# Two-layer hybrid block on one core: the next norm two tiles behind the update, other weight places and product order in the last groups, and norms in place

## The chip, the cores and the metric

One NeuronCore of one Trainium2 chip runs the whole program. The metric is the device time of one execution in microseconds (us). A core has five engines with queues of their own: PE (TensorE, matrix products), DVE (VectorE), ACT (ScalarE), POOL (GpSimd) and SP (SyncE, which here issues every DMA). [...] PE's clock stands at one of two levels, which the profile shows as a granted clock of 1.0 or 0.5.

## The reference

The input is 1024 tokens of width 1024, everything in float32. Each of two layers computes a mixer and an MLP, both with adaptive norms:

```
mod = cond @ w_ada[l] + b_ada[l]; sh_m, sc_m, g_m, sh_f, sc_f, g_f = split(mod, 6)
h = rmsnorm(x, norm_g[l, 0]) * (1 + sc_m) + sh_m
y = hybrid_mixer(h, ...)            # three attention-like branches, joined, @ w_out
x = x + g_m * rmsnorm(y, norm_g[l, 1])
h = rmsnorm(x, norm_g[l, 2]) * (1 + sc_f) + sh_f
y = square(relu(h @ w_up[l])) @ w_down[l]        # 1024 -> 4096 -> 1024
x = x + g_f * rmsnorm(y, norm_g[l, 3])
```

A norm of a token needs the sum of squares over its 1024 columns, so it is a reduction, a reciprocal root and a product.

## The kernel before

**Arithmetic.** A float32 product is made of three PE matmuls (`mm3`, lines 191 to 193): each operand is cut into a high part (a cast, mostly on ACT) and a low part (what is left, a subtraction, mostly on DVE), and high·high, high·low and low·high are added up in PSUM. `split` (lines 234 and 235) makes the two parts of a weight or an activation.

**Order of the work.** The kernel is written as Python generators that are woven together (`weave`), and a scheduler at build time then sets each engine's instruction order from the data dependences, the order written and its own timeline. On the chip each engine takes its queue strictly in order. SP issues the DMAs in order too; a DMA whose target is not yet free holds up all behind it.

**Memory.** Three kinds of space matter. The arena F (`Arena`, about 17 slabs of 128x1024 words) holds loads and intermediate tiles; a slab can be filled again when its last reader is done. The tile R is cut into slots ("places") of 2x1024 columns for split operands: in the down projection `load` takes places from the list `free`, in other stages R holds the normed and transposed input `hT` (slots 8 to 15). PSUM is used as named banks: `bank_s` with two buffers in the down projection, `bank_t` for transposes there, `bank_b` in the projections.

**Stages of a layer.** Eight token tiles of 128 tokens, t = 0 to 7. The mixer ends with `out_proj` per tile (load of x, line 1296; sum of squares; product; line 1302 stores x) and `renorm` per tile: load x (line 1317) into one slab, square it into a second slab u (line 613), the norm product into u (line 614), then transposes on PE and splits into `hT` (lines 620, 621, or 210 to 235 in `transp_late` for tiles 4 to 7, which also forms the sums that the up projection uses). Tiles 6 and 7 keep their x on the chip (`kept`). The up projection `mlp_up` works on weight columns in 16 blocks: six "lead" loads of 128 columns (`plain`) run while tiles 4 to 7 are still being normed; then come loads of 256 columns (line 269), whose sums POOL forms (lines 277 to 283) and `split` cuts, five products each (`sums`).

**The down projection** (`mlp_down`) goes through the 32 slices of 128 rows in groups, `GROUPS = [2] + [4] * 6 + [2, 4]`. For each slice of a group it loads and splits a piece of the activations and a piece of the weights (two places), then for each tile multiplies all slices of the group into one PSUM tile of two halves and adds that to y[t] (line 386; in the last group the last tile in halves, line 381). Group 7 has two slices (four places) and group 8, the last, four slices (eight places). Before either of them the list `free` is sorted.

**The end of a layer** is in `finish` of `run` (line 1498) and `finish` of the class: for each tile of the last group a square on ACT (line 666), the reciprocal root (lines 182 to 186), a product on DVE (line 667), the residual addition on POOL (line 668) and the store. Tile 7 goes in halves, with the addition on DVE (lines 656 to 664). In layer 0 the norm for layer 1 follows the addition: square (line 613 again), root, product (line 614), then the transposes (lines 641 and 630). `load_w` (lines 693 and 694) splits the first weights of layer 1 for the queries and keys; their projection is the first `bank_b` product of the layer. The names `fss` and `nss` in the rows are the sums of squares of the finish and of the norm.

## Time and profile before

| what | us |
|---|---|
| median of three runs (lowest, highest) | 2834.05 (2823.96, 2837.48) |
| the profiled execution | 2822.46 |
| its span in the trace | 2820.4 |
| PE busy in it | 2621.0 |
| DVE busy in it | 1747.9 |
| ACT busy in it | 1134.2 |
| POOL busy in it | 576.7 |

The rows of the trace give a start and a duration in us from the span's start. A number in square brackets at a row's end is the idle time of that engine just before, with the engine and line that ended it. Matmuls overlap: one of 512 columns is shown with 0.39 us, but the next one starts 0.23 later at full clock. Where a row says x8, eight instructions are merged, and its duration runs from the first start to the last end. In the profiled execution layer 0's down projection ends near 1459, layer 1's mixer near 2090, and its down projection near 2812.

### The profile page before, as it was taken

To read this page: it belongs to the slowest core of one execution; us is meant where nothing else is said; L and a number is where in the kernel's file an instruction comes from. 1 tells how busy PE (TensorE), PEld (TensorE's weight loads), DVE (VectorE), ACT (ScalarE), POOL (GpSimd) and SP (SyncE) were. 2 spreads that over 40 slices of the span, in tenths; PEclk is the share of its full clock that TensorE was granted. 3 is DMA by queue.
4 is the path that set the end of the run, shared out by engine and by line. 5 is a ranking of instruction groups with operands and counts; after the bars stand their busy time and mean duration, and the time that the engine had idled before them with its cause. 6 is when DMAs were issued, how large, how long until landed. Compare 5 with 4: busy or idle time off the path is not lost. (4 is left out here: it accounts for less than half of the span.)

```text
span 2820.4 us, 34988 instructions
## 1 busy us (share of the span) xinstructions
PE 2621.0 (93%) x12530; PEld 2048.1 (73%) x12530; DVE 1747.9 (62%) x3351; ACT 1134.2 (40%) x2265; POOL 576.7 (20%) x509
## 2 busy tenths in 40 slices
PE   5799998898799999999979999979987999999998
PEld 4677776675677777777768777657765888888886
DVE  7767676643887777576574667754458555543435
ACT  5243443544544445121153434444446455621112
POOL 1441243210143320000021113341002433000002
PEclk9899999998999999999989999879998999999999
DMA  6441312313255547353240222231132433531303
GB/s 226 116 137 49 96 60 77 98 62 104 79 185 172 160 158 236 129 166 116 78 148 22 64 84 66 61 119 60 59 120 83 146 116 112 194 134 60 120 30 120
DMA packets 268529, 311.55 MB, mean 110 GB/s; under 512 B 28674, under 2 KB 212164, under 8 KB 268356
## 3 DMA queue, kind: packets, MB, share of 16 engines
q1 hardware_dynamic: 268356, 309.32, 34.0%
q8 instruction: 99, 1.62, 0.2%
q14 instruction: 74, 0.61, 0.1%
HBM read 242.85 MB, written 66.43 MB: 110 GB/s over the span
## 5 line engine op out<-in xcount | busy, mean ns | idle before, releaser
L191 PE MATMUL bank_b<-split 128*128 128x512 f32 (+2 forms) x1824 | 722.9, 397 | 47.1 <-ACT split L234 28.1
L192 PE MATMUL bank_b<-split 128*128 128x512 f32 (+2 forms) x1824 | 707.5, 388 | 0.2 <-DVE split L694 0.2
L193 PE MATMUL bank_b<-split 128*128 128x512 f32 (+2 forms) x1824 | 704.8, 388 | 1.2 <-DVE split L636 1.2
L234 ACT CAST split<-arena_f 128x512 fp32r<-128x512 f32 (+1 forms) x384 | 281.8, 761 | 630.9 <-PE bank_s L192 385.9
L191 PE MATMUL bank_s<-split 128*128 128x512 f32 (+2 forms) x1152 | 454.1, 397 | 17.9 <-ACT split L1061 4.7
L192 PE MATMUL bank_s<-split 128*128 128x512 f32 (+2 forms) x1152 | 450.8, 391 | 9.6 <-DVE split L235 6.7
L193 PE MATMUL bank_s<-split 128*128 128x512 f32 (+2 forms) x1152 | 448.2, 389 | 0.0
L191 PEld LDWEIGHTS bank_b<-split 128*128 128x128 f32 x1824 | 352.5, 193 | 126.9 <-ACT split L234 32.2
L235 DVE TENSOR_TENSOR split<-arena_f,split 128x512 fp32r<-128x512 f32 (+1 forms) x384 | 355.2, 941 | 89.7 <-ACT split L234 88.2
L193 PEld LDWEIGHTS bank_b<-split 128*128 128x128 f32 x1824 | 350.7, 192 | 68.4 <-issue 3.1
L192 PEld LDWEIGHTS bank_b<-split 128*128 128x128 f32 x1824 | 352.4, 193 | 63.8 <-issue 3.9
L386 DVE TENSOR_TENSOR arena_f<-arena_f,bank_s 128x1024 f32<-128x1024 f32 x126 | 153.5, 1219 | 248.4 <-PE bank_s L193 248.2
L191 PEld LDWEIGHTS bank_s<-split 128*128 128x128 f32 (+1 forms) x1152 | 218.1, 190 | 73.5 <-issue 5.8
L192 PEld LDWEIGHTS bank_s<-split 128*128 128x128 f32 (+1 forms) x1152 | 218.9, 190 | 56.8 <-DVE split L235 9.0
L193 PEld LDWEIGHTS bank_s<-split 128*128 128x128 f32 (+1 forms) x1152 | 218.9, 190 | 44.3 <-issue 0.8
L869 ACT ACTIVATE arena_f<-bank_s,nm 128x128 f32<-128x128 f32 (+3 forms) x192 | 141.9, 741 | 188.6 <-DVE nm L868 155.2
L868 DVE TENSOR_REDUCE nm<-bank_s 128x1 f32<-128x128 f32 (+3 forms) x192 | 141.5, 751 | 106.2 <-PE bank_s L1083 62.1
L548 DVE SCALAR_TENSOR_TENSOR arena_f<-arena_f,cond 128x128 f32<-128x128 f32 x448 | 155.9, 376 | 50.5 <-DMA arena_f<-in_w_ada 20.7
L897 ACT COPY arena_f<-bank_t 128x512 f32<-128x512 f32 (+1 forms) x160 | 86.7, 542 | 108.9 <-PE bank_t L894 97.9
L668 POOL TENSOR_TENSOR arena_f<-arena_f 128x1024 f32<-128x1024 f32 x14 | 34.5, 2461 | 460.9 <-DVE arena_f L667 453.9
L250 ACT ACTIVATE arena_f<-arena_f 128x512 f32<-128x512 f32 x128 | 80.8, 632 | 113.7 <-DVE arena_f L324 52.5
L881 PE MATMUL bank_a<-arena_f 128*64 128x256 f32 (+1 forms) x640 | 108.3, 399 | 19.2 <-ACT arena_f L897 15.0
(280 smaller groups left out, 3260.1 us busy)
## 6 DMA issues: line engine op xcount, KB each, us to landing
arena_f<-in_w_ada SPq DMA_DIRECT2D x80, 512.0 KB
d_r<-arena_f SPq DMA_DIRECT2D x128, 256.0 KB
arena_f<-in_w_up SPq DMA_DIRECT2D x32, 1024.0 KB
arena_f<-in_w_down SPq DMA_DIRECT2D x64, 512.0 KB
arena_f<-d_r SPq DMA_DIRECT2D x64, 512.0 KB
arena_f<-d_x SPq DMA_DIRECT2D x36, 512.0 KB
d_x<-arena_f SPq DMA_DIRECT2D x23, 512.0 KB
arena_f<-in_w_in SPq DMA_DIRECT2D x20, 512.0 KB
```

Of the source, the lines that this page charges most:

```text
L191: mm(out, wh, xh, start=start, stop=False)
L192: mm(out, wh, xl, start=False, stop=False)
L193: mm(out, wl, xh, start=False, stop=stop)
L234: self.nc.scalar.copy(hi, src)
L235: (eng or self.nc.vector).tensor_sub(lo, src, f32(hi))
L250: nc.scalar.activation(t, t, AF.Relu)
L386: nc.vector.tensor_add(y[t], y[t], ps)
L548: nc.vector.scalar_tensor_tensor(acc, in0=w[:, k], scalar=self.cond[:, k:k + 1], in1=acc, op0=ALU.mult, op1=ALU.add)
L868: nc.vector.tensor_reduce(nm, S[:, 0:n], axis=AX.X, op=ALU.max, negate=True)
L869: nc.scalar.activation(p[:, 0:n], S[:, 0:n], AF.Exp, bias=nm, accum_out=ls)
L881: nc.tensor.matmul(bk[jj * 64:jj * 64 + 64, 128 * half:256], v[:, 2 * c + jj], e[:, 256:384] if half else e[:, jj * 256:jj * 256 + 256], s ...
L897: nc.scalar.copy(held, ps[:, 0:w])
```

## The change

Three parts. In `mlp_down` the two sorts of `free` give other places to the last two groups: group 7 now takes 0, 1, 6, 7, and group 8 takes 2, 3, 4, 5 first and then 0, 1, 6, 7; and in the last group the products of tiles 6 and 7 run as first slices of 6, first slices of 7, last slices of 6, last slices of 7. In `run` the finish of tile t is written ahead of the norm, and the norm is that of tile t-2 instead of t-1. In `renorm` x is loaded into u itself and normed there, and the squares, which nobody reads, go to a free part of R; tiles 6 and 7 hand over their two slabs.

```
@@ -365,20 +365,35 @@
             last = f0 == FF // P
             if f0 + GROUPS[-1] >= FF // P:
 
-                free.sort()
+                free.sort(key=lambda i: (i > 7, i in (0, 1, 6, 7)) if last else (i > 7, 1 < i < 6))
             rw = []
             for f in fs:
                 rw.append((load(self.d_r[l][f]), load(w_dn[f * P:(f + 1) * P, :])))
-            for t in range(NT):
+            banks = {}
+
+            def products(t, ns, tip=False):
                 tok = slice(t * P, t * P + P)
-                ps = self.bank2()
-                tip = last and t == NT - 1
+                ps = banks[t] = banks.get(t) or self.bank2()
                 for dh in range(2):
                     dd = slice(dh * 512, dh * 512 + 512)
-                    for n, ((_, r), (_, wd)) in enumerate(rw):
+                    for n in ns:
+                        r, wd = rw[n][0][1], rw[n][1][1]
                         self.mm3(ps[:, dd], r[:, 0, tok], r[:, 1, tok], wd[:, 0, dd], wd[:, 1, dd], n == 0, n == size - 1)
                     if tip:
                         nc.vector.tensor_add(y[t][:, dd], y[t][:, dd], ps[:, dd])
+
+            for t in range(NT):
+                tip = last and t == NT - 1
+                if not last or t < NT - 2:
+                    products(t, range(size))
+                elif not tip:
+
+                    for tt in (t, t + 1):
+                        products(tt, range(size // 2))
+                    products(t, range(size // 2, size))
+                else:
+                    products(t, range(size // 2, size), True)
+                ps = banks[t]
                 if g == 0:
                     y.append(F.get(D, top=True))
                     nc.scalar.copy(y[t], ps)
@@ -606,11 +621,14 @@
         return t
 
 
-    def norm(self, x, a, xn):
+    def norm(self, x, a, xn, junk=None):
 
         nc = self.nc
         ss = self.sm(1, "nss")
-        nc.scalar.activation(xn, x, AF.Square, accum_out=ss)
+        if junk is None:
+            nc.scalar.activation(xn, x, AF.Square, accum_out=ss)
+        else:
+            nc.scalar.activation(junk, x.rearrange("p (a k q) -> p a k q", a=2, q=P), AF.Square, accum_out=ss)
         nc.vector.scalar_tensor_tensor(xn, in0=x, scalar=self.rstd(ss), in1=a, op0=ALU.mult, op1=ALU.mult)
 
     def cut_cols(self, ps, b, hi, lo):
@@ -1300,23 +1318,24 @@
         nc.vector.scalar_tensor_tensor(u, in0=u, scalar=rs, in1=g, op0=ALU.mult, op1=ALU.mult)
         nc.vector.tensor_add(x, x, u)
         nc.sync.dma_start(dst[t * P:t * P + P], x)
-        F.put(u)
         if keep is None:
+            F.put(x, u)
+        else:
+            keep[t] = x, u
+
+    def renorm(self, t, src, nxt, hT):
+
+        F = self.F
+        if type(src) is dict:
+            x, u = src[t]
+            self.norm(x, nxt[0], u)
             F.put(x)
         else:
-            keep[t] = x
-
-    def renorm(self, t, src, nxt, hT):
-
-        F = self.F
-        u = F.get(D)
-        if type(src) is dict:
-            x = src[t]
-        else:
-            x = F.get(D)
-            self.nc.sync.dma_start(x, src[t * P:t * P + P])
-        self.norm(x, nxt[0], u)
-        F.put(x)
+
+            u = F.get(D)
+            self.nc.sync.dma_start(u, src[t * P:t * P + P])
+            h = self.R[:, 8 * SLOT:16 * SLOT].rearrange("p (a k t) -> p a k t", a=2, k=KD)
+            self.norm(u, nxt[0], u, h[:, :, 4:8, t * P:t * P + P])
         yield 1.0
         if t < 4:
             self.transp8(u, hT[0], hT[1], t, True, nxt[1])
@@ -1504,14 +1523,14 @@
                         tail["w"] = list(self.stage_w(I["w_in"][l + 1], self.qk_cols(0), 2))
                 if more and t == NT - 1:
                     tail["w0"] = self.load_w(tail["w"], 2)
+                if t < NT:
+                    self.finish(y[t], self.d_x[2 * l], tail["g"], o, t, tail["x"][t % 3], y[t],
+                                hT[0][:, :, t * P:t * P + P])
+                if more and t > 1:
+                    self.norm(tail["x"][(t - 2) % 3], tail["nxt"][0], y[t - 2])
                 if more and 2 < t < 7:
                     self.transp8(y[t - 3], hT[0], hT[1], t - 3, False, tail["nxt"][1])
                     F.put(y[t - 3])
-                if more and 0 < t <= NT:
-                    self.norm(tail["x"][(t - 1) % 3], tail["nxt"][0], y[t - 1])
-                if t < NT:
-                    self.finish(y[t], self.d_x[2 * l], tail["g"], o, t, tail["x"][t % 3], y[t],
-                                hT[0][:, :, t * P:t * P + P])
 
             bg = iter(())
             if more:
@@ -1525,6 +1544,7 @@
                 F.put(tail["g"])
                 if more:
                     finish(NT)
+                    finish(NT + 1)
                     for t in range(4, NT):
                         self.transp8(y[t], hT[0], hT[1], t, True, tail["nxt"][1])
                         F.put(y[t])

```

Line numbers move: in the rows of the changed kernel 401 and 383 are what 386 and 381 were, 685 is 667, 632 is 614, 639 is 621, 712 is 694, 680 and 681 are 662 and 663, 1336 is 1317, 1314 and 1320 are 1296 and 1302.

On DVE, at the end of layer 0, where tiles 2 and 3 are added. L386 (401) adds the products to y, L667 (685) is the product of the finish, L614 (632) that of the norm; the `rstd` names tell which root a product uses. Before:

```order
L186 TENSOR_SCALAR rstd_y_10688<-rstd_t_10690,rstd_y_10688 128x1
L386 TENSOR_TENSOR arena_f<-arena_f,bank_s 128x1024
L186 TENSOR_SCALAR rstd_y_10700<-rstd_t_10702,rstd_y_10700 128x1
L614 SCALAR_TENSOR_TENSOR arena_f<-arena_f,rstd_y_10688 128x1024
L667 SCALAR_TENSOR_TENSOR arena_f<-arena_f,rstd_y_10700 128x1024
L386 TENSOR_TENSOR arena_f<-arena_f,bank_s 128x1024
```

The norm product of tile 0 stands ahead of the finish product of tile 1, behind the add of tile 2. The same place with the change:

```order
L186 TENSOR_SCALAR rstd_y_10729<-rstd_t_10731,rstd_y_10729 128x1
L186 TENSOR_SCALAR rstd_y_10742<-rstd_t_10744,rstd_y_10742 128x1
L685 SCALAR_TENSOR_TENSOR arena_f<-arena_f,rstd_y_10729 128x1024
L632 SCALAR_TENSOR_TENSOR arena_f<-arena_f,rstd_y_10742 128x1024
L401 TENSOR_TENSOR arena_f<-arena_f,bank_s 128x1024
```

The finish product is now that of tile 2, one tile further on, and the norm product of tile 0 follows right behind it, ahead of the add of tile 3.

On SP, at the seam from the mixer to the up projection of layer 1. `d_x` is x in memory, `in_w_up` the weights: 128x8x128 a lead load, 128x8x256 a load for the sums; `d_r` takes the up projection's results. Before:

```order
L1317 DMA arena_f<-d_x_106 128x1024 x3
L1296 DMA arena_f<-d_x_105 128x1024 x2
L1317 DMA arena_f<-d_x_106 128x1024
L269 DMA arena_f<-in_w_up 128x8x128 x3
L1317 DMA arena_f<-d_x_106 128x1024
L1302 DMA d_x_106<-arena_f 128x1024
L269 DMA arena_f<-in_w_up 128x8x128
L1302 DMA d_x_106<-arena_f 128x1024
L252 DMA d_r_110<-arena_f 128x512 x2
L269 DMA arena_f<-in_w_up 128x8x128 x2
L252 DMA d_r_110<-arena_f 128x512 x3
L269 DMA arena_f<-in_w_up 128x8x256
```

The last two lead loads stand behind two stores of results, and the first load for the sums behind three more. With the change:

```order
L269 DMA arena_f<-in_w_up 128x8x128
L1314 DMA arena_f<-d_x_105 128x1024
L1336 DMA arena_f<-d_x_106 128x1024 x2
L1314 DMA arena_f<-d_x_105 128x1024
L1336 DMA arena_f<-d_x_106 128x1024 x2
L269 DMA arena_f<-in_w_up 128x8x128 x2
L1320 DMA d_x_106<-arena_f 128x1024
L269 DMA arena_f<-in_w_up 128x8x128
L1320 DMA d_x_106<-arena_f 128x1024
L269 DMA arena_f<-in_w_up 128x8x128
L252 DMA d_r_110<-arena_f 128x512 x2
L269 DMA arena_f<-in_w_up 128x8x128
```

Five of the six lead loads now stand ahead of the first store of results, and directly behind the sixth follow two loads for the sums.

On DVE, at the end of the kernel, where tile 6 is finished and tile 7 is added in halves (L381, with the change L383). Before:

```order
L386 TENSOR_TENSOR arena_f<-arena_f,bank_s 128x1024
L183 TENSOR_SCALAR rstd_m_20456<-fss_20453 128x1
L381 TENSOR_TENSOR arena_f<-arena_f,bank_s 128x512
L184 RECIPROCAL rstd_y_20455<-rstd_y_20455 128x1
L185 TENSOR_SCALAR rstd_t_20457<-rstd_y_20455,rstd_m_20456 128x1
L186 TENSOR_SCALAR rstd_y_20455<-rstd_t_20457,rstd_y_20455 128x1
L667 SCALAR_TENSOR_TENSOR arena_f<-arena_f,rstd_y_20455 128x1024
L381 TENSOR_TENSOR arena_f<-arena_f,bank_s 128x512
```

The first half of tile 7 is added in the middle of tile 6's finish. With the change:

```order
L401 TENSOR_TENSOR arena_f<-arena_f,bank_s 128x1024
L183 TENSOR_SCALAR rstd_m_20469<-fss_20466 128x1
L184 RECIPROCAL rstd_y_20468<-rstd_y_20468 128x1
L185 TENSOR_SCALAR rstd_t_20470<-rstd_y_20468,rstd_m_20469 128x1
L186 TENSOR_SCALAR rstd_y_20468<-rstd_t_20470,rstd_y_20468 128x1
L685 SCALAR_TENSOR_TENSOR arena_f<-arena_f,rstd_y_20468 128x1024
L383 TENSOR_TENSOR arena_f<-arena_f,bank_s 128x512 x2
```

Both halves of tile 7 are added behind tile 6's whole finish. On PE the second half's last six matmuls wait for the first half's add.

## Rows read from the trace of the kernel before

**Rows 1.** The page of the profile: busy time by engine with its share of the span, and the chain that ended last, by engine.

```profile
PE 2621.0 (93%) x12530; PEld 2048.1 (73%) x12530; DVE 1747.9 (62%) x3351; ACT 1134.2 (40%) x2265; POOL 576.7 (20%) x509
...
PE 31%; DVE 3%; DMA 2%; ACT 1%; issue 1%; POOL 0%; DVEq 0%; SPq 0%; ACTq 0%; POOLq 0%
```

**Rows 2.** Busy time in five stretches: start and end, length, then each engine's busy time with the number of instructions, PE's granted clock, the DMA share and GB/s. The first runs from tile 0's add in layer 0's last group to the first projection of layer 1, the second is its later part from tile 6's add on.

```profile
1418.60:1483.40 64.80, 45.25 (x213) 37.70 (x212) 52.47 (x119) 35.98 (x89) 20.81 (x9) 0.86 0.39 125
1452.20:1483.40 31.20, 11.65 (x57) 9.79 (x55) 29.31 (x66) 18.86 (x50) 11.90 (x6) 0.71 0.46 144
1410.90:1414.30 3.40, 3.40 (x8) 2.65 (x9) 2.10 (x2) 0.00 (x0) 0.00 (x0) 0.50 0.98 282
2796.00:2806.00 10.00, 10.00 (x46) 8.29 (x45) 6.01 (x12) 2.66 (x6) 3.93 (x3) 1.00 0.50 183
2106.00:2171.00 65.00, 54.39 (x240) 43.19 (x239) 54.95 (x132) 39.86 (x91) 9.66 (x6) 0.93 0.21 69
```

**Rows 3.** The timeline of PE at the start of group 7: in layer 0 (first row) and in layer 1.

```profile
1386.94 0.50 PE L192 MATMUL bank_s<-split 128*128 128x512 f32 x1 [1.16 <-DVE split L235]
...
2739.59 0.73 PE L191 MATMUL bank_s<-split 128*128 128x512 f32 x2 [0.50 <-ACT split L234]
...
2741.99 0.50 PE L192 MATMUL bank_s<-split 128*128 128x512 f32 x1 [0.98 <-DVE split L235]
```

**Rows 4.** The timeline at the start of group 8: PE, ACT and DVE in layer 0, and PE's second wait in layer 1.

```profile
1408.38 0.73 PE L191 MATMUL bank_s<-split 128*128 128x512 f32 x2 [1.18 <-ACT split L234]
1410.79 0.74 PE L192 MATMUL bank_s<-split 128*128 128x512 f32 x1 [1.67 <-DVE split L235]
...
1406.33 3.89 ACT L234 CAST split<-arena_f 128x1024 fp32r<-128x1024 f32 x4 [20.14 <-PE bank_s L192]
...
1408.38 4.62 DVE L235 TENSOR_TENSOR split<-arena_f,split 128x1024 fp32r<-128x1024 f32 x4
...
2765.82 0.69 PE L192 MATMUL bank_s<-split 128*128 128x512 f32 x1 [1.67 <-DVE split L235]
```

**Rows 5.** The timeline from layer 0's last group to layer 1's first projection: DVE, then POOL, then PE.

```profile
1429.85 1.27 DVE L614 SCALAR_TENSOR_TENSOR arena_f<-arena_f,rstd_y 128x1024 f32<-128x1024 f32 x1
...
1450.33 1.53 DVE L621 SCALAR_TENSOR_TENSOR split<-bank_t,arena_f,split 128x128 fp32r<-128x128 f32 x4
1452.17 1.22 DVE L386 TENSOR_TENSOR arena_f<-arena_f,bank_s 128x1024 f32<-128x1024 f32 x1 [0.31 <-PE bank_s L193]
...
1459.53 3.00 DVE L694 TENSOR_TENSOR split<-arena_f,split 128x1024 fp32r<-128x1024 f32 x1
...
1432.45 2.40 POOL L668 TENSOR_TENSOR arena_f<-arena_f 128x1024 f32<-128x1024 f32 x1 [6.54 <-DVE arena_f L667]
1441.82 2.40 POOL L668 TENSOR_TENSOR arena_f<-arena_f 128x1024 f32<-128x1024 f32 x1 [6.96 <-issue]
...
1459.04 2.42 POOL L694 TENSOR_TENSOR split<-arena_f,split 128x848 fp32r<-128x848 f32 x1 [6.14 <-ACT split L693]
...
1472.57 1.94 PE L630 MATMUL bank_s<-ident,arena_f 128*128 128x128 f32 x8 [12.79 <-DVE arena_f L614]
...
1481.76 1.97 PE L630 MATMUL bank_s<-ident,arena_f 128*128 128x128 f32 x8 [5.72 <-DVE arena_f L614]
```

**Rows 6.** The timeline of PE from the mixer to the up projection in layer 0: the first output product of tile 6, a product of a lead load, and the first product of the sums.

```profile
703.88 0.80 PE L191 MATMUL bank_b<-split 128*128 128x512 f32 x1 [3.10 <-ACT split L635]
...
771.14 0.80 PE L191 MATMUL bank_b<-split 128*128 128x512 f32 x1 [10.43 <-ACT split L234]
...
788.12 0.50 PE L191 MATMUL bank_b<-split 128*128 128x512 f32 x1 [2.60 <-ACT split L234]
```

**Rows 7.** The timeline of the same seam in layer 1: PE (a lead product, the first product of the sums), SP's issue of the first load for the sums, and DVE on the late transposes of tile 7.

```profile
2140.30 0.50 PE L191 MATMUL bank_b<-split 128*128 128x512 f32 x1 [3.01 <-ACT split L234]
...
2179.06 0.79 PE L191 MATMUL bank_b<-split 128*128 128x512 f32 x1 [8.17 <-ACT split L234]
...
2168.93 0.38 SPq L269 DMA_DIRECT2D arena_f<-in_w_up  x1
...
2171.00 2.16 DVE L220 SCALAR_TENSOR_TENSOR arena_f<-bank_s,arena_f 128x128 f32<-128x128 f32 x8 [1.76 <-PE bank_s L210]
...
2175.75 4.83 DVE L235 TENSOR_TENSOR split<-arena_f,split 128x512 fp32r<-128x512 f32 x3
```

**Rows 8.** The timeline at the end of the kernel: DVE from tile 5's add to the last products, and PE's restart in tile 7.

```profile
2799.95 1.22 DVE L386 TENSOR_TENSOR arena_f<-arena_f,bank_s 128x1024 f32<-128x1024 f32 x1 [0.63 <-PE bank_s L193]
...
2803.47 1.28 DVE L667 SCALAR_TENSOR_TENSOR arena_f<-arena_f,rstd_y 128x1024 f32<-128x1024 f32 x1
2805.39 1.22 DVE L386 TENSOR_TENSOR arena_f<-arena_f,bank_s 128x1024 f32<-128x1024 f32 x1 [0.63 <-PE bank_s L193]
...
2808.11 0.69 DVE L381 TENSOR_TENSOR arena_f<-arena_f,bank_s 128x512 f32<-128x512 f32 x1
...
2811.91 0.69 DVE L381 TENSOR_TENSOR arena_f<-arena_f,bank_s 128x512 f32<-128x512 f32 x1 [1.15 <-PE bank_s L193]
...
2814.71 1.42 DVE L662 SCALAR_TENSOR_TENSOR arena_f<-arena_f,rstd_y 128x512 f32<-128x512 f32 x2
2816.05 1.29 DVE L663 TENSOR_TENSOR arena_f<-arena_f 128x512 f32<-128x512 f32 x2
...
2808.86 0.50 PE L191 MATMUL bank_s<-split 128*128 128x512 f32 x1 [0.78 <-DVE arena_f L381]
```

## The prediction

> **What bounds the kernel now.** I read the page's first part and its chain first: TensorE is busy 93% of the span, and the chain that ended last runs over PE far more than over any other engine [rows 1]. So only time in which PE stands idle or runs at a lower clock can be won, and the share says little: it is an average over dense stretches and a few seams. Next I listed PE's idle stretches on the timeline around the places that the diff touches. There are five: the start of the last two groups of the down projection, once per layer [rows 3, 4]; the seam from layer 0's last group to layer 1's first projection, with PE idle for 12.79 and 5.72 us just before it [rows 5]; the seam from the mixer to the up projection in layer 0 [rows 6] and in layer 1 [rows 7]; and the end of the kernel [rows 8]. Last, the windows tell what runs there: in the 64.8 us from tile 0's add to the first projection of layer 1 VectorE is busy 52.47 us, and in the last 31.2 of them it is busy nearly throughout, beside 11.65 of PE [rows 2]. So VectorE all but bounds that seam, and a wait that goes there hands over to VectorE's queue.
>
> **Entry of the last two groups (places of the weights).** Group 7 (two slices) had to wait until group 6 had read places 2 and 3; now it takes places free since group 5. Its waits, 1.16 us in layer 0 and 0.50 + 0.98 in layer 1 [rows 3], should go: 2.6 us. Group 8 had two waits, 1.18 and 1.67, because its first two places are those that group 7 has just read; then 8 matmuls at half clock in 3.40 us [rows 2, 4]. Now its first two slices lie in places 2 to 5, ready early, and PE has the two slices of tile 0 and of tile 1 (first half) to run, 14 matmuls of 0.23 (46 in 10 us, counting those cut at either edge [rows 2]), before it needs the last places. ScalarE's four casts take 3.89 and VectorE's four subtractions 4.62 us from about the same point [rows 4]; 3.2 us of matmuls stand against the second subtraction (2.3 us after the first starts), and 6 more against the fourth, so I leave about 1.2 us of waiting. Gain per layer 2.85 - 1.2 = 1.65, and 8 x (0.43 - 0.23) = 1.6 of clock. Layer 1 shows the same stall [rows 4]. Two layers: 6.5. Together 9.1 us, between 2.6 (group 8 waits as before) and 12 (nothing waits); 4.4 of it is layer 0's.
>
> **Seam of the layers (norm two tiles behind).** Before, the norm of tile t-1 stood ahead of the finish of t on VectorE, and waited there for POOL's 2.40 us addition and a square: POOL's additions came 9 us apart, a tile's products take 5.4 [rows 5, 8]. That wait goes. What comes next is VectorE's own work. From tile 6's add (1452.17) to the first projection are 31.2 us [rows 2, 5]. Counted in the two orders, between that add and the last split that the projection needs there stand now 12 more of the 128x128 splits at about 0.35 to 0.38 (1.53 for four), 2 more norm products at 1.27, one finish product fewer, and tile 7's four half-width operations at 1.42 + 1.29 [rows 5, 8]: 4.2 + 2.6 - 1.3 + 2.7 = 8.2 us. Tile 6's add itself comes 12 matmuls later, 2.7 us, since 12 of tile 7's were put ahead of its second half. So the projection would start 10.9 us later after tile 0's add than before. Against it: the gaps that VectorE had in those 31.2 us, some 2 [rows 2], one more tile's transposes that PE has done by then (8 in 1.97 [rows 5]), and a part of the slowed weight splits (3.00 for one [rows 5]). I take +6 us, a loss; the ends are +11 and -13 (the larger idle stretch goes entirely and VectorE keeps up).
>
> **Mixer to up projection (renorm in place).** Nothing is added: the same instructions, one buffer fewer per norm, so loads of x and of w_up are issued earlier. In layer 1 the first load for the sums was issued at 2168.93, when tile 7's norm product ended, and PE waited 8.17 us to 2179.06 [rows 7]; by the order it waits now for a transpose of tile 6 instead. Late next is VectorE's split of the second sum, done when the next starts at 2175.75: 3.4 us to win. The lead load behind the 3.01 gap at 2140.30 [rows 7] also goes earlier: 3.0. I take -6, ends 0 and -11.2 (both stretches whole). In layer 0 there are idle stretches of 3.10, 10.43 and 2.60 [rows 6]; the sixth lead load still waits for the same sum of tile 5, and the first load for the sums now waits for a split in the late transposes of one tile more; such a tile's took VectorE 9.6 us in layer 1, from 2171.00 to 2180.58 [rows 7]. Against that the output projection of tile 6 (behind the 3.10) may start earlier, its cast no longer behind three squares that wait for loads; by how much no row shows, and I set it equal: 0, ends -9 and +9.
>
> **The end of the kernel.** Before, tile 7's first half was added at 2808.11, ahead of tile 6's finish product, and its second half at 2811.91. Now tile 6's add comes 2.7 us later (2805.4 + 2.7 = 2808.1), both half adds stand behind tile 6's whole finish, and PE's last six matmuls wait for the first of them. A finish takes 4.8 us from the add's start to its product's end (2799.95 to 2804.75) [rows 8]: 2812.9. From the first half add's start to PE's restart it was 0.75, and from there over 12 matmuls to the second half add 3.05; six fewer take 1.4 less. So the second half add starts at 2815.3, +3.4 us. Ends 0 (the last six don't wait) and +4.6 (they run at half clock).
>
> **Sum.** -9.1 + 6 + 0 - 6 + 3.4 = -5.7 us. The profiled execution took 2822.46, span 2820.4 and 2.1 around it, so 2816.8 on its scale; the median of the three runs is 2834.05, 11.6 above it, and on that scale, in which the result comes, it is 2828. A measurement of this kernel tells about 0.5%, 14 us, from no change; the three runs lie 13.5 apart.
>
> **Rivals.**
> The seam opens (chance 0.2). The norms no longer hold up the finish, and VectorE's small splits overlap as closely as they do in its fullest stretches; then the 12.79 us go and the seam is -13 instead of +6: -24.7, 2809. For it: VectorE has 12.3 us to spare in the window. Against: nearly all lies in the first half, where PE sets the pace and VectorE has nothing queued [rows 2].
>
> POOL blocks VectorE (chance 0.2), the slower side. The norm product now stands straight behind the finish product that releases POOL's addition, four times, and once two weight splits and it. In the trace a VectorE split with both inputs in SBUF that started 0.49 us after a POOL operation took 3.00 us [rows 5], and three splits of 512 beside POOL took 4.83 [rows 7], where a lone one of 1024 takes 1.15 (4.62 for four [rows 4]). If POOL gets in first, VectorE loses up to 2.40 each time: +12 in a seam that VectorE bounds; and the earlier loads put POOL's sums beside the late splits of layer 1, 2.8 us each for two: +17.6 in all, so 2828 + 17.6 = 2846. It decides if POOL starts before the queued norm product. Against: that product waits for nothing once the finish product ends, while POOL waits for a signal of it, so VectorE should be first, and POOL's delay is hidden by two tiles of slack.
> The Trainium skill (SBUF — State Buffer, SBUF: two separate sides) says that a VectorE operation with two SBUF inputs and a GpSimd operation exclude each other for a whole instruction, and that who starts first keeps the port. By that rule it is this race that decides, 0 or +12, and the slowed rows agree with it; no row before shows a norm product right behind a finish product.
>
> The loads gain nothing (chance 0.2): renorm in place issues loads earlier, but PE's gaps in layer 1 stay, since VectorE's late transposes end no sooner. For it: VectorE is busy 54.95 of 65 us there [rows 2]. Then the sum is about 0, 2834.
>
> **How the numbers follow.** The forecast with its own range of 2816 to 2840 has 0.4. Faster by over 0.5%: most of the first rival (0.17) and the fast edge of the forecast (0.12): 0.29. Slower by over 0.5%: half of the second (0.11) and edges of the others (0.06): 0.17. Within: 0.54. The range is 2808 to 2849: it holds the first rival's value at its low end and the second's, and the larger ends of the seam and of layer 0 are left out.
>
> **What would show it.** Entry: in the changed profile no PE wait at the start of group 7, at group 8 waits of together about 1.2 us and no clock of 0.5 behind them. Seam: from tile 0's add to the first projection 69 to 75 us instead of 64.8, VectorE nearly without idle time in the last 35; POOL's additions about 5.5 to 7 us apart at first. If norm products beside POOL last 2 to 3.6 us, the second rival is right; if the projection starts within 60 us, the first. Layer 1: PE's idle stretch before the sums about 5 us instead of 8.17, and not ended by a load. End: PE idle some 4 to 5 us before its last six matmuls. What would make it wrong is above all VectorE's pace in the seam, the largest term that the trace before does not show, and a change of layer 0's seam by its full bound.

## The result: slower by 0.5%, and the profile after

The changed kernel takes 2841.97 us (median of 20 runs, 2826.68 to 2856.61) where the kernel before takes 2828.27 (20 runs, 2813.86 to 2839.72): ratio 1.005, interval 1.0033 to 1.0068, some 14 us slower. The profiled execution of after has a span of 2837.3, 16.9 more than the one of before, so it shows a typical loss.

The page of after, to be read beside [rows 1]: busy time, and the chain that ended last.

```profile
PE 2642.7 (93%) x12530; PEld 2064.6 (73%) x12530; DVE 1746.6 (62%) x3351; ACT 1134.9 (40%) x2265; POOL 575.7 (20%) x509
...
PE 63%; DVE 11%; DMA 8%; issue 2%; ACT 2%; POOL 1%; SPq 0%; DVEq 0%; ACTq 0%; POOLq 0%
```

PE is busy 21.7 us longer with the same 12530 matmuls, so it is not more work: more of them run at the lower clock (mean granted clock 0.953, before 0.958). The chain could be followed further back than in before (its shares add up to 87% instead of 38%), so its shares can't be compared; DMA has 8% in it, where before's chain shows 2%. The page doesn't say where the time went. For that both traces were laid side by side by the number of the matmul: the time from the start of one numbered matmul to that of a later one is a stage, and the table gives how much longer (+) or shorter each stage is than in the first profile of before. "Again" is a second profile of before's code, so its column is what an execution varies by. In what follows A is the part on places and product order, B the norm two tiles behind, C the norms in place. A number names the same work only where the built order is the same: in most of these kernels the scheduler also gave PE another order in layer 1's mixer.

| stage (length before, us) | again | after | C alone | A and B |
|---|---|---|---|---|
| layer 0 mixer (673) | +3.5 | -1.7 | -3.5 | +2.1 |
| its end to the up projection (143) | +1.1 | +5.3 | +4.6 | -0.3 |
| up projection (264) | -1.4 | +8.2 | +9.9 | -0.4 |
| start of the down projection (88) | +0.4 | +5.7 | +4.9 | +3.0 |
| entry of groups 7 and 8 (75) | -0.7 | -4.8 | -0.1 | -4.4 |
| seam to layer 1 (97) | -0.5 | +7.8 | +5.1 | +4.3 |
| layer 1 mixer (514) | -4.2 | +8.4 | +1.7 | -1.0 |
| its end to the up projection (160) | +0.3 | -10.4 | -6.9 | -0.1 |
| start of the down projection (69) | +0.2 | +3.3 | +3.5 | +0.6 |
| entry of groups 7 and 8 (86) | 0.0 | -4.8 | -0.1 | -4.8 |
| last tiles (28) | 0.0 | +0.6 | 0.0 | +0.6 |

The dense stages left out agree to about a microsecond. In C alone the seam and layer 1's mixer have to be read together, +6.8: this build has the mixer's first attention products 75 matmuls earlier in PE's order, and the 5.1 arises there, behind the first projection. The loss that the prediction didn't see lies in layer 0 between the mixer and the down projection: 19.2 us. Two more rows have no term in the prediction: layer 1's mixer (+8.4, left open at the end) and the start of its down projection (+3.3; 1.4 to 5.1 in the seven kernels with C in both layers, at most 0.6 in those without C).

**Entry of the last groups.** The timeline of after at the start of group 8: PE in layer 0, PE in layer 1, then ACT and DVE in layer 0.

```profile
1425.93 0.50 PE L192 MATMUL bank_s<-split 128*128 128x512 f32 x1 [0.27 <-DVE split L235]
1428.20 0.50 PE L192 MATMUL bank_s<-split 128*128 128x512 f32 x1 [0.62 <-DVE split L235]
...
2785.48 0.50 PE L192 MATMUL bank_s<-split 128*128 128x512 f32 x1 [0.27 <-DVE split L235]
2787.75 0.50 PE L192 MATMUL bank_s<-split 128*128 128x512 f32 x1 [0.61 <-DVE split L235]
...
1421.47 3.91 ACT L234 CAST split<-arena_f 128x1024 fp32r<-128x1024 f32 x4 [18.57 <-PE bank_s L192]
...
1423.52 4.62 DVE L235 TENSOR_TENSOR split<-arena_f,split 128x1024 fp32r<-128x1024 f32 x4
```

Instead of 1.18 and 1.67 [rows 4] PE waits 0.27 and 0.62, and the waits at group 7 [rows 3] are gone from both layers. What is left is VectorE's four subtractions, 4.62 us as before, that PE runs into. The stretch around it has a granted clock of 1.00, where before 8 matmuls ran at 0.50 [rows 2].

**Seam to layer 1.** Busy time from tile 0's add to the first projection, and in its later part (columns as in [rows 2]).

```profile
1431.74:1502.72 70.98, 48.06 (x214) 38.74 (x212) 63.11 (x145) 41.26 (x106) 27.15 (x9) 0.81 0.43 140
1457.00:1502.72 45.72, 22.80 (x99) 17.77 (x97) 43.16 (x101) 27.45 (x74) 16.67 (x6) 0.71 0.49 153
```

71.0 us instead of 64.8, with VectorE busy 43.16 of the last 45.72. The timeline there: DVE (finish products L685, norm products L632, tile 6's add L401, the half add L383, tile 7's half-width additions L681), POOL (additions L686, a part of a weight split L712), PE.

```profile
1438.45 2.70 DVE L685 SCALAR_TENSOR_TENSOR arena_f<-arena_f,rstd_y 128x1024 f32<-128x1024 f32 x1
...
1445.88 1.28 DVE L632 SCALAR_TENSOR_TENSOR arena_f<-arena_f,rstd_y 128x1024 f32<-128x1024 f32 x1
...
1463.05 1.22 DVE L401 TENSOR_TENSOR arena_f<-arena_f,bank_s 128x1024 f32<-128x1024 f32 x1 [0.42 <-PE bank_s L193]
...
1472.06 0.67 DVE L383 TENSOR_TENSOR arena_f<-arena_f,bank_s 128x512 f32<-128x512 f32 x1
...
1491.36 1.28 DVE L681 TENSOR_TENSOR arena_f<-arena_f 128x512 f32<-128x512 f32 x2
1492.56 3.04 DVE L632 SCALAR_TENSOR_TENSOR arena_f<-arena_f,rstd_y 128x1024 f32<-128x1024 f32 x1
...
1437.67 2.40 POOL L686 TENSOR_TENSOR arena_f<-arena_f 128x1024 f32<-128x1024 f32 x1 [64.90 <-DVE rstd_m L183]
...
1446.04 3.39 POOL L686 TENSOR_TENSOR arena_f<-arena_f 128x1024 f32<-128x1024 f32 x1 [2.37 <-DVE arena_f L685]
...
1491.30 3.22 POOL L712 TENSOR_TENSOR split<-arena_f,split 128x848 fp32r<-128x848 f32 x1 [7.74 <-ACT split L711]
...
1472.78 0.75 PE L191 MATMUL bank_s<-split 128*128 128x512 f32 x1 [4.80 <-DVE arena_f L383]
1478.57 1.06 PE L648 MATMUL bank_s<-ident,arena_f 128*128 128x128 f32 x8 [2.91 <-DVE arena_f L632]
1484.96 1.97 PE L659 MATMUL bank_t<-ident,arena_f 128*128 128x128 f32 x8 [5.32 <-DVE split L639]
```

The two long idle stretches of before [rows 5] have become six of 1.3 to 5.3 us, each ended by VectorE. Where the norm product starts first (1445.88, POOL at 1446.04), VectorE keeps its 1.28 and POOL pays one microsecond (3.39 instead of 2.40); where POOL starts first (1437.67), VectorE pays: 2.70 instead of 1.28. The Trainium skill (SBUF — State Buffer, SBUF: two separate sides) says that the first to start keeps the port for its instruction; the trace agrees, with these two pairs of rows. At 1491.30 POOL and VectorE's L681 start within 0.06 us of each other; POOL's operation takes 3.22 instead of 2.42 [rows 5], L681 its usual 1.28, and the norm product behind them 3.04.

**Mixer to up projection, layer 0.** The timeline of after: PE, the load for the first sums on SP, the first sum on POOL and its cast on ACT; then the next load of the stream that computes layer 1's modulation (`w_ada`, called the mod stream below), and what it holds up.

```profile
768.16 0.80 PE L193 MATMUL bank_b<-split 128*128 128x512 f32 x1 [5.21 <-DVE split L235]
791.72 0.79 PE L191 MATMUL bank_b<-split 128*128 128x512 f32 x1 [9.60 <-ACT split L234]
...
782.76 2.40 SPq L269 DMA_DIRECT2D arena_f<-in_w_up  x2
...
788.41 1.26 POOL L277 TENSOR_TENSOR arena_f<-arena_f 128x512 f32<-128x512 f32 x1 [17.64 <-DMA arena_f<-in_w_up]
...
789.70 0.62 ACT L234 CAST split<-arena_f 128x512 fp32r<-128x512 f32 x1 [3.50 <-POOL arena_f L277]
...
848.97 0.56 SPq L548 DMA_DIRECT2D arena_f<-in_w_ada  x1
...
855.52 2.49 DVE L563 SCALAR_TENSOR_TENSOR arena_f<-arena_f,cond 128x128 f32<-128x128 f32 x2 [7.22 <-DMA arena_f<-in_w_ada]
857.93 0.67 DVE L327 TENSOR_TENSOR arena_f<-arena_f,bank_b 128x512 f32<-128x512 f32 x1
...
858.75 0.77 PE L191 MATMUL bank_b<-split 128*128 128x512 f32 x1 [3.72 <-DVE arena_f L327]
```

The first sums load is issued at 782.76 and POOL starts on it 5.65 us later; everything behind it follows, and PE stands 9.60 where it stood 2.60 before its first product of the sums; the 10.43 ahead of that has become 5.21 [rows 6]. Before, that load was the first of these two:

```profile
776.59 1.01 SPq L269 DMA_DIRECT2D arena_f<-in_w_up  x2
```

So it comes 6.2 us later. What SP waited for just ahead of it: before (767 to 778 us), then after (744 to 783 us; total, times, longest).

```profile
SPq L269 <- DVE arena_f L614: 9.7, 1, 9.7
```

```profile
SPq L559 <- DVE split L235: 12.6, 1, 12.6
SPq L269 <- DVE split L235: 4.5, 1, 4.5
```

Before, the load waited for a norm product (L614). Now a small load of the mod stream (L559) ahead of it waits 12.6 us for a split on VectorE, and then the load itself 4.5 for another split.

Further on VectorE stands 7.22 us at the head of its queue for a mod load issued only 6.55 before, and the up projection's own operation L327, queued behind it, comes late for PE. SP's waits from 780 to 1000 us, before, then after:

```profile
SPq L533 <- DVE arena_f L548: 14.0, 10, 2.9
```

```profile
SPq L548 <- DVE arena_f L563: 34.1, 13, 5.3
```

This is one and the same wait, 14.0 us before and 34.1 after: the mod stream's load waits until a mod step has read the slab. The arena gives out the free slab with the oldest return, by the order in which the program is written. C takes one slab fewer per norm, so from there on loads get other slabs than before, and some get one whose last reader comes late; SP's queue holds all loads behind them.

**Start of layer 0's down projection.** ACT waits for the first weights, and PE for ACT's copy out of PSUM, which stands behind the casts.

```profile
1097.60 1.05 ACT L234 CAST split<-arena_f 128x1024 fp32r<-128x1024 f32 x1 [5.71 <-DMA arena_f<-in_w_down]
1105.52 1.04 ACT L234 CAST split<-arena_f 128x1024 fp32r<-128x1024 f32 x1 [2.67 <-DMA arena_f<-in_w_down]
...
1109.51 0.80 PE L191 MATMUL bank_s<-split 128*128 128x512 f32 x1 [4.95 <-ACT arena_f L399]
```

Before, PE's longest wait there is 1.19 us.

**Mixer to up projection, layer 1.** PE's idle stretches before the sums, to be read beside [rows 7]: 3.66 and 2.91 instead of the 8.17, and instead of the 3.01 at a lead product nothing longer than 1.06.

```profile
2178.01 0.50 PE L191 MATMUL bank_b<-split 128*128 128x512 f32 x1 [1.06 <-ACT split L234]
...
2194.41 0.79 PE L191 MATMUL bank_b<-split 128*128 128x512 f32 x1 [3.66 <-ACT split L234]
2198.11 1.22 PE L191 MATMUL bank_b<-split 128*128 128x512 f32 x2 [2.91 <-ACT split L234]
```

**The end.** DVE from tile 6's add on, and PE's restart, beside [rows 8].

```profile
2821.63 1.22 DVE L401 TENSOR_TENSOR arena_f<-arena_f,bank_s 128x1024 f32<-128x1024 f32 x1 [0.63 <-PE bank_s L193]
...
2826.35 0.68 DVE L383 TENSOR_TENSOR arena_f<-arena_f,bank_s 128x512 f32<-128x512 f32 x1
2828.78 0.69 DVE L383 TENSOR_TENSOR arena_f<-arena_f,bank_s 128x512 f32<-128x512 f32 x1 [1.75 <-PE bank_s L193]
...
2827.09 0.50 PE L191 MATMUL bank_s<-split 128*128 128x512 f32 x1 [1.42 <-DVE arena_f L383]
```

Tile 6's add to tile 7's second half add: 7.15 us, before 6.52.

### The profile page after: what moved, and what is told of

Read it like the earlier page. It is cut to its first block, busy times and chain, and to the rows that moved or that the text cites. A ratio compares the mean times of both kernels' runs of the same rounds, so it can differ in the third digit from the quotient of the medians.

```text
span 2837.3 us, 34952 instructions
## 1 busy us (share of the span) xinstructions
PE 2642.7 (93%) x12530; PEld 2064.6 (73%) x12530; DVE 1746.6 (62%) x3351; ACT 1134.9 (40%) x2265; POOL 575.7 (20%) x509
## 4 chain that ended last, share of the span: by engine, by line
PE 63%; DVE 11%; DMA 8%; issue 2%; ACT 2%; POOL 1%; SPq 0%; DVEq 0%; ACTq 0%; POOLq 0%
PE bank_b L191 10%; PE bank_b L193 9%; PE bank_b L192 9%; PE bank_s L191 8%; PE bank_s L192 8%; PE bank_s L193 8%; PE bank_a L899 2%; PE bank_s L952 2%; DVE split L235 2%; DMA arena_f<-in_w_ada 2%; PE bank_t L912 2%; DVE arena_f L563 2%; DMA arena_f<-in_w_up 1%; DMA d_r<-arena_f 1%; PE bank_b L1046 1%
## 5 line engine op out<-in xcount | busy, mean ns | idle before, releaser
L401 DVE TENSOR_TENSOR arena_f<-arena_f,bank_s 128x1024 f32<-128x1024 f32 x126 | 153.6, 1219 | 237.5 <-PE bank_s L193 237.4
L887 ACT ACTIVATE arena_f<-bank_s,nm 128x128 f32<-128x128 f32 (+4 forms) x192 | 141.9, 741 | 179.9 <-DVE nm L886 157.4
L952 PE MATMUL bank_s<-split 32*128 32x512 f32 (+3 forms) x576 | 119.2, 378 | 11.1 <-ACT arena_f L887 8.8
L686 POOL TENSOR_TENSOR arena_f<-arena_f 128x1024 f32<-128x1024 f32 x14 | 37.8, 2700 | 445.4 <-DVE rstd_m L183 408.6
```

Of the source, the lines that this page charges most:

```text
L401: nc.vector.tensor_add(y[t], y[t], ps)
L887: nc.scalar.activation(p[:, 0:n], S[:, 0:n], AF.Exp, bias=nm, accum_out=ls)
L952: nc.tensor.matmul(S[mp][:, c0:c1], Q[rw, a, tok], K[rw, b, c0:c1], start=a == b, stop=a == 1 and c1 < n)
```

## Experiments

All ratios are to the kernel before, run beside them on the same chip, with the 95% interval. The stages are those of one profiled execution.

### Which part costs: A, B, C and pairs

**A alone** (the diff of `mlp_down` only).

> Only the places of the last two groups and the order of the last group's products; norm order and renorm as before. The theory that the loss belongs to renorm in place: nothing moves before layer 0's group 7; the two entries give 4.4 to 4.8 us each as they did in the changed kernel (lag there fell from 16.4 to 11.6 and from 20.7 to 15.9), the end of the kernel costs 1 to 3; together -6 to -8 us, and layer 1's mixer within 2 us of before. The rival, that any new order at the seam costs layer 1's mixer about 8 us (lag 19.4 to 27.4 in the changed kernel): about 0 in all, with those 8 us in layer 1's mixer here too.

2804.23 us (four executions), 0.9913 (0.9881 to 0.9946). More than expected: the entries give 9.1, the rest lies in layer 1's mixer (-8.7 in this profile) and the way to its up projection (-6.2).

**B alone** (the diff of `run` only).

> Only the norm two tiles behind the finish. My prediction's mechanism (VectorE bounds the seam): the first projection of layer 1 starts 3 to 8 us later after tile 0's add than the 64.8 us of before, nothing moves before layer 0's last group, the up projections and layer 1's transition stay: +3 to +8 us. The rival (the seam opens without the reordered products): the projection starts earlier than 60 us after tile 0's add, -5 to -12 us.

2834.18, 1.0015 (0.9993 to 1.0037): no change that could be told. Its seam is 4.1 us longer, and no other stage gains over 1 us; layer 1's mixer is 10.0 longer in this profile, which the ratio doesn't bear out.

**C alone** (the diffs of `norm`, of `renorm` and of what hands over to it).

> Only renorm in place. If it holds the loss: in layer 0 the sums start 3 to 4 us later with the first load for the sums issued about 783, 5 to 8 us more go in the up projection between 850 and 950, about 5 at the start of layer 0's down projection (the lag reaches +17 by 1150), layer 1's transition gives back 8 to 11, and about 3 go at layer 1's down projection: +9 to +13 us in all. If the loss is of the seam and of layer 1's mixer instead: under +3 us here.

2842.65, 1.0059 (1.0037 to 1.0081). C alone is as slow as the whole change, and the table shows its loss in after's stages: 4.6, 9.9 and 4.9 in layer 0.

**A and B without C.**

> Places, products and the norm two behind, renorm as before. Theory (renorm in place holds the loss): entries -9, seam +6 to +7, end +1 to +3, layer 1's transition unchanged: -2 to +1 us. Rival (seam and mixer hold it): +5 to +8 us, with a later first projection and about 8 us in layer 1's mixer.

2816.75, 0.9965 (0.9936 to 0.9994): faster than before, though less so than A alone (the two intervals just overlap). So C makes the result. The parts don't add up: A is worth 24 us alone, but C with A and B (1.005) is no faster than C alone (1.0059).

**The kernel before once more**, unchanged, for the spread of a profile.

> The kernel before, unchanged, for a second trace: how far a stage moves between two executions of one program. If the stages of layer 1's mixer are as steady as the dense ones, the lags there agree with the first trace within 2 us; if the 14 us that the kernel with places and products alone won in layer 1's mixer are an accident of one execution, this trace differs there by 5 us or more. The start of layer 0's down projection, 2.3 to 3.0 us later in three kernels that change nothing before it, should come 2 to 3 later here too if the first trace was an early one.

2821.34, one execution; the column "again" above. Layer 1's mixer moves by 4 us without any change.

### In which layer C costs

**C in layer 0 only**, and **C in layer 1 only, tiles 0 to 5** (tiles 6 and 7 as before). `place` is `l == 0` in the one and `l == 1 and t < 6` in the other:

```diff
+        if place:
             if type(src) is dict:
                 x, u = src[t]
...
+        else:
+            u = F.get(D)
```

> Renorm in place in layer 0 alone. Theory (layer 0 holds the loss, since the first load for the sums waits there for a split of the late transposes, and loads of the adaptive weights come late in the up projection): layer 0's part as with both layers, a lag of about +15 us by 1150, layer 1's transition unchanged (0 instead of -9.6): +13 to +20 us. Rival (layer 0's part is small and the loss lies in layer 1): under +5 us.

2843.78, 1.0055 (1.0029 to 1.0081): as slow as C in both layers. Its three stages from layer 0's mixer on are at +2.6, +6.3 and +4.7.

> Renorm in place in layer 1 alone, and there for tiles 0 to 5 (tiles 6 and 7 keep x alone, as before). Theory: nothing moves before 2060; the transition to the up projection gains 5 to 10 us, since the first load for the sums no longer waits for tile 7's norm product; the start of layer 1's down projection may lose up to 3.5: -3 to -9 us. Rival (the gain of the transition belongs to tiles 6 and 7): 0 to -2 us.

2820.49, 0.9983 (0.9956 to 1.001), with the way to layer 1's up projection 10.8 us shorter, as in after, though layer 1's mixer, which this edit doesn't touch, was 11.2 longer in this profile. So the loss is in the main layer 0's, and the prediction's gain is layer 1's: it shows in its stage, while this ratio can't be told from no change.

**A with C in layer 1 only.**

> Places and products together with renorm in place in layer 1 alone (tiles 0 to 5). If the parts add up: -21 of places and products and -3 to -9 of the transition, -24 to -30 us. If what places and products won in layer 1's mixer hangs on an order that the scheduler doesn't repeat: -10 to -18 us.

2804.0 (four executions), 0.9925 (0.9901 to 0.9948): no slower than A alone, and no faster.

### Why C costs in layer 0: the late loads

**C, with the first sums load taken and issued ahead of the late norms:**

```diff
+            if not plain and ahead:
+                st = ahead.pop(0)
...
         for i in range(LEAD):
+            if i == 0:
+                ahead.append(F.get(KD, 2 * P))
+                dma(ahead[0], w_up[:, :, 0:2 * P])
```

> Renorm in place in both layers, as in the run of it alone, with one edit more: the first load of weights for the sums is given its place and issued ahead of the late norms, so that it can't wait for a split of the late transposes. Theory: in layer 0 the idle stretch of 8 to 10 us before the first product of the sums, ended by that load, goes or shrinks to the 3 us that the splits allow, the lag after it is 4 to 7 us smaller than in renorm alone (which is 17 us slower than before); total +8 to +13 us. Rival (VectorE's late splits set that start anyway): the stretch stays with another releaser and the total at +15 to +19.

2833.47, 1.0041 (1.0021 to 1.0061). The stage to the up projection goes from +4.6 to -9.5; PE's 9.60 before the sums is gone. These are its idle stretches at the last lead product and at the first products of the sums:

```profile
778.69 0.79 PE L191 MATMUL bank_b<-split 128*128 128x512 f32 x1 [4.00 <-ACT arena_f L313]
787.28 0.50 PE L191 MATMUL bank_b<-split 128*128 128x512 f32 x1 [0.35 <-ACT arena_f L313]
```

That load was therefore the cause in this stage. The two stages behind it shrink too, the up projection from +9.9 to +3.2 and the start of the down projection from +4.9 to +0.6. The kernel is still slower than before; layer 0's mixer, which this edit doesn't touch, was 16 us longer in the profile.

**C, with the mod stream's loads issued one step further ahead of their use:**

```diff
         if lag is None:
+            yield
             for k in range(8):
```

> Renorm in place in both layers, and the loads of the adaptive weights that run beside the two MLP stages issued one step of that stream earlier. Theory: of the 10 us that renorm alone lost in layer 0's up projection, the part in which VectorE's queue waited for such a load (up to 7.5 us at once, PE 4.1 behind it) goes: the up projection's lag grows by 3 us or less instead of 10, the total falls from +17 to about +10. Rival (those loads are late because VectorE is late): the lag grows by 8 to 10 as before and the total stays at +15 to +19.

2835.8, 1.0034 (1.0008 to 1.006). Now the stage to the up projection stays at +5.4, but the up projection itself falls from +9.9 to +2.5 and the start of the down projection from +4.9 to -0.9. So this edit leaves the first of the three stages and heals the two behind it, while the one before heals the first and most of the others: the up projection's loss is not of the mod loads alone. The ratios of either edit by itself (1.0041 and 1.0034) can't be told from that of C alone (1.0059); only the stages show what each does.

**The whole change with the first load ahead; the same without B; A alone with the first load ahead:**

> The whole change, with the first load of weights for the sums issued ahead of the late norms. Theory: as renorm with that load ahead was 14 us better in layer 0's transition and 9 in its median, the changed kernel goes from +14 to +0..+5 us against before.

2828.4, 0.9995 (0.9972 to 1.0018), with layer 0's three stages at -7.2, +4.0 and +1.0.

> The same without the norm two behind: places, products, renorm in place, first load ahead. Theory (the norm two behind costs the seam 4 to 6 us): 4 to 6 us faster than the whole change with that load ahead, about -5 to +1 against before if renorm still costs its up projection, down to -20 if it doesn't. Rival (the norm two behind pays once the loads are early): the same or slower than with it.

2829.91, 1.0005 (0.9985 to 1.0026), the stages at -7.1, +3.4 and +0.8: B neither costs nor gives here.

> Places and products and the first load ahead, renorm and norm as before. Places and products alone were 21 us faster than before; if the early load gains in layer 0's transition (10.43 and 2.60 us of idle PE there before) without renorm in place, -25 to -33 us; if it only moves the wait to the lead loads, -15 to -22.

2808.98, 0.994 (0.9916 to 0.9965), no better than A without it. Issuing the load earlier is no gain by itself: without C the stage to the up projection is at +0.4 in this profile, and the up projection was 8.9 longer. It takes back what C lost.

**The whole change with both loads ahead:**

> The whole change with both loads earlier: the first load for the sums ahead of the late norms, and those of the adaptive weights one step earlier. Theory (the change lost by two loads that came late in layer 0, 5 + 8 + 5 us, and its other parts gain 9 at the entries and 6 to 10 in layer 1's transition against 8 at the seam): the transition of layer 0 at -7, its up projection at +3 or less, the start of the down projection within 1; in all -10 to -18 us against before. Rival (the loads only hand the wait on to layer 1's mixer and down projection): 0 to -5.

2813.76, 0.9951 (0.9933 to 0.9969): the same change is now faster than before, and faster than with the first load alone (0.9995). It is not faster than A and B without C (0.9965) or A alone (0.9913): with its two loads repaired C costs nothing that could be told, and gives nothing. PE's timeline at the last lead product and the first products of the sums:

```profile
777.91 0.80 PE L191 MATMUL bank_b<-split 128*128 128x512 f32 x1 [4.25 <-ACT arena_f L313]
786.51 0.50 PE L191 MATMUL bank_b<-split 128*128 128x512 f32 x1 [0.51 <-ACT arena_f L313]
```

Layer 0's three stages are at -8.6, -0.3 and -1.3, where after has +5.3, +8.2 and +5.7. The profile is of the slowest of this kernel's eleven executions (2833.73) and 11.4 us longer than before's: layer 0's mixer has +14.7 in it (see the last section) and layer 1's +15.6. In the up projection (790 to 1050 us) the granted clock is 1.00; first this kernel, then after:

```profile
790.00:1050.00 260.00, 255.02 (x1110) 199.54 (x1109) 202.82 (x399) 121.94 (x218) 94.11 (x81) 1.00 0.52 166
```

```profile
790.00:1050.00 260.00, 247.93 (x1054) 193.86 (x1055) 190.96 (x379) 112.88 (x198) 84.14 (x80) 0.97 0.50 156
```

### What in A gives the time

**The two sorts alone**, with the product order of before:

> Only the places of the last two groups; products in the order of before, norm and renorm as before. The entries give 4.4 and 4.8 as with the product order. If the 14 us that places and products won in layer 1's mixer come with the places (they alter the order there too): -21 to -25 us. If they come with the order of the products: -8 to -11 us. The end of the kernel and the seam between the layers as before.

2822.68, 0.9984 (0.9964 to 1.0005). The entries gain 4.4 and 4.7 us in full. The table's seam is 5.9 longer here and layer 1's mixer 6.4 shorter, both for the reason given for C alone: the first projection comes as early as in the next kernel (1477.9 and 1478.2 us), and behind it this build has the first attention products 75 matmuls earlier in PE's order.

**A with the new product order in layer 0 only:**

```diff
-                if not last or t < NT - 2:
-                    products(t, range(size))
+                if not last or t < NT - 2 or l + 1 == DEPTH:
+                    products(t, range(size), tip)
```

> Places in both layers, the order of the last group's products changed in layer 0 alone. By my prediction's term for the end of the kernel (+3.4 for the reordered products there) this is 3 us faster than places and products in both layers, -24 us; by the traces since (the lag moved by 0.5 to 1 after the last group) it is the same within 1 us, -21.

2809.53, 0.9947 (0.9927 to 0.9968). So the order in layer 0 is worth something beside the places: 13 us between the medians, though the intervals just overlap. Where, is not shown: the two kernels differ mostly in seam and mixer taken together (-5.1 here, -0.5 with the sorts alone), where the scheduler also built another order.

## Why the prediction was wrong

The forecast was 6 us faster, within the noise; the time came 14 slower. 2841.97 lies within the range, and "slower by over 0.5%" had 0.17.

- **Entry of the last groups: right.** -9.1 predicted, -9.6 measured, with 0.89 us of waiting left where 1.2 was reckoned. The sorts alone bring it.
- **Seam: right in its size, by two steps that cancel.** +6 predicted, 71.0 - 64.8 = +6.2 measured (the table's +7.8 is of a stage that runs on past the first projection). From tile 6's add to the projection it is 39.7 instead of 31.2, +8.5, where VectorE's extra work was put at 8.2. The step "tile 6's add itself comes 12 matmuls later" failed: from tile 0's add to tile 6's it is 31.3 us instead of 33.6. And the gaps that VectorE was to fill were no help: two of its products lost 1.4 and 1.8 us beside POOL (its weight splits lost about as much there as before).
- **End of the kernel: mis-sized.** +3.4 predicted, +0.6 measured, from the same step. Tile 6's add follows tile 5's by 5.44 us in both kernels, and behind it PE runs 18 matmuls before its wait and 6 after it, so tile 7's first slices don't stand ahead of tile 6's last: on PE the order as built has all 24 matmuls of tile 6 and then those of tile 7. I had taken the order from the source, not from the built program.
- **Mixer to up projection, layer 1: the mechanism was right, the size too small.** -6 predicted, -10.4 measured, inside the bound of -11.2; C in layer 1 alone shows it too (-10.8). Not all of the size need be C's: A alone has -6.2 in this stage, but it keeps a wait of 8.49 us before the sums.
- **Mixer to up projection, layer 0: the step that failed.** "I set it equal: 0" came out at +5.3, inside its ends. The load for the sums does wait for a split of the late transposes, as the text said; its price was the larger idle stretch before the sums. But the sum ended there. "Nothing is added: ... loads of x and of w_up are issued earlier" was taken to hold for all loads. Giving up a slab changed which slab every later load fills, and the up projection (+8.2) and the start of the down projection (+5.7, of which 2 to 3 also come in profiles of kernels without C) had no term. C alone, C in layer 0 alone, and the two edits that move those loads show it. These three stages are 19.2 of the 23 us between forecast and profile; what is left is the balance of the other rows, of which layer 1's mixer (+8.4) stays open.
- **The rivals.** The seam did not open. POOL did not take VectorE's time in the way priced: the norm products behind finish products started first, four of four that could be read, and only two products lost 1.4 and 1.8 us; that rival's time, 2846, is close to the result for another reason. "The loads gain nothing" is refuted in layer 1.

Left open: why A alone is worth 24 us by its ratio, when the entries give 9. The profiles put the rest into layer 1's mixer (-8.7 with A alone, -11.0 with C in layer 1 beside it, -4.5 with the order of layer 0 only), but that stage moves by -4 to +11 in executions of code that has before's order there, so one profile each doesn't settle it. For the same reason a third cost of C is open: layer 1's mixer is longer than before in all seven profiles with C in both layers (+1.7 to +15.6) and shorter in all six with A and without C in layer 0 (-1.0 to -11.0), and in all thirteen PE's built order there differs from before's in over 200 of some 2550 matmuls. Nor was the mod stream's longer lead tried without C, so how much of the 0.9951 is a gain of its own is not known. That the arena's choice of slabs is what made the loads late is read from its code and from SP's waits; no run kept the slabs fixed while C was in.

## What to carry to other kernels

With a queue that issues loads in order into rotating buffers, a buffer given up is a change to every load behind it: before pricing it, list what each of the next loads will wait for, to the end of the next stage and not only at the edit. If an in-place edit costs where nothing was edited, look at the load queue's waits for a reader that has become late, and take those loads' buffers earlier; here that turned 0.5% slower into 0.5% faster, which is where the kernel stands without the in-place edit too. And take the position of instructions from the built order: two steps here were read from the source and the scheduler had undone them.

## What the runs showed of the hardware

Two things had not been expected. The same code can lose some 14 us by PE's clock alone. Layer 0's mixer was 13.7, 16.2, 15.0 and 14.7 us longer in four profiles whose edits don't touch it (C in layer 1 only, C and A with the first load ahead, the whole change with both loads ahead), nearly all of it in one quarter of the stage, while the dense stages agree to a tenth of a microsecond in most. The longest of these stretches, in before (360 to 380 us), then in the whole change with both loads ahead (340 to 360, 360 to 380):

```profile
360.00:380.00 20.00, 19.46 (x102) 14.52 (x101) 17.73 (x40) 8.81 (x21) 10.04 (x8) 1.00 0.25 74
```

```profile
340.00:360.00 20.00, 20.00 (x115) 14.62 (x113) 15.71 (x38) 9.89 (x24) 4.72 (x4) 0.99 0.27 84
360.00:380.00 20.00, 20.00 (x62) 14.97 (x62) 14.93 (x36) 7.01 (x16) 7.29 (x6) 0.50 0.19 63
```

PE is shown busy without a break both ahead of the fall and in it, so this is no wait: the granted clock is 0.50 instead of 1.00, and 62 matmuls run where 102 did. In the four profiles it is 0.50 to 0.62 from 360 to 380, in before 1.00; why it fell in these executions and not in the others, no row shows. And a POOL addition that starts behind a VectorE product of the same size costs POOL about 1.0 us (3.39 for 2.40), while a VectorE product behind a POOL operation pays up to 1.8 (3.04 for 1.28): in these rows the later one pays roughly what is left of the earlier.
